# Moving the first burst of level products of the recurrence from index 52 to index 26 of its stage

## The chip, the cores and the metric

The kernel runs on one core of a Trainium2 chip. The metric is device time in microseconds (us) of one execution; several executions of the same program are timed and their median is compared. A profile of one execution shows when each instruction ran on each engine: PE (TensorE, the matrix engine; its weight loads are listed as PEld), DVE (VectorE), ACT (ScalarE), POOL (GpSimd) and SP (SyncE, which issues most transfers).

## The reference

The reference is one layer of a streaming encoder on a sequence of 256 positions and a model width of 1,024, in fp32. In order: a feed-forward block, a mixing block, a cross-attention to a memory of 256 positions, and a second feed-forward block, each with RMS norms and a residual. The change lies in the mixing block. One input projection makes the inputs of two branches. Branch A is a gated linear recurrence over 8 heads of 128 by 128 state:

```
def step(state, xs):
    qt, kt, it, bt = xs
    diff = bt[:, :, :, None, :] - bt[:, :, None, :, :]
    decay = jnp.exp(jnp.where(mask, diff, -jnp.inf))
    a = jnp.einsum('bhtd,bhsd,bhtsd->bhts', qt, kt, decay)
    o_intra = jnp.einsum('bhts,bhsv->bhtv', a, it)
...
o_a = rmsnorm(o_a.astype(x.dtype), hg_norm_g[l]) * jax.nn.silu(g_a)
```

Each score of query t and key s is weighted, channel by channel, by the product of the gates f between s and t. Branch B is an attention with a forget gate per head, whose logits f_b are eight columns of the same input projection. Both branches are projected, gated, added and projected out.

## The kernel before, in words

**Products in three parts.** An fp32 matrix product is made of three products of a reduced type: every operand is split into a high part and a low part. A weight tile (128 x 1024, or 128 x 688 for the columns spoken of here) is brought by SP into one of four buffers called raw; ACT rounds it into a tile called hi (line 145); DVE makes lo = raw - hi (line 147). SP can load the next tile into a raw buffer once DVE has made lo of the tile that was in it. hi and lo have eight buffers each.

**The stage of the change.** From about 252 us the kernel multiplies the normalized input by the columns of g_a and f_b (the loop at line 1023). They come in three groups of 344 columns, each of four weight tiles; a group is made for two halves of the positions, 24 products each, so the stage has 6 x 24 = 144 products of 128 x 344. They are indexed from 0 behind the mark r0. At the end of each half ACT makes a sigmoid (tile z, line 1030) and DVE multiplies it into G (line 1031). The two accumulators (tiles named mm) alternate, so a half can begin when DVE has made G of the half before the last one. Behind the stage come the products of k_b and q_b with 128 x 1024 weight tiles.

**Level products.** In the same time the recurrence is prepared. Its score matrix is built from levels: level 0 holds blocks of 1, and level m pairs blocks of m positions whose distance is covered by a product of gates. For two groups of four heads (class Rec, line 878) four methods act on a level: products (line 901) issues many small matrix products on PE, 32 x 32 or 32 x (2 x 16); grow (line 952) multiplies gates into the tiles k and qf on DVE (line 970) and combines gates (line 980), with copies on ACT of the early halves of k (gather, tile early, line 946) and of the later halves of qf (stash, into tile q, line 950); keep (line 990) copies the wanted part of the products into aux on DVE (lines 994 and 999) or on ACT. POOL clears parts of f after the first grow.

**Order.** Instructions of an engine run in the order in which they stand. The level work is taken out of the program order by hand: `after(i)` places all that it holds behind the matrix product with index i, with high priority, and a scheduler puts the ACT, DVE and POOL instructions into their queues accordingly. The levels come in six bursts, SETS = (0, 1), (2, 4), (8, 16), (32), (64), (128), and R_AT holds their six places:

```
for si, ms in enumerate(SETS):
    with after(r0 + R_AT[si]):
```

The first burst holds the products of levels 0 and 1 for both groups of heads (96 small products in the program; each is two matrix instructions, and each of these has a weight load), the grow of level 1 and the keep of both levels. The grow of level 2 stands behind the G of the second group's first half (R_GROW) whatever R_AT is.

Of the kernel before, what the change touches and what calls it, by code (L numbers as in the profile page):

```python
# [50 lines left out]
M_T = (106, 119)  # L51
M_O = (136, 140)

R_AT = (52, 126, 210, 252, 286, 318)

R_GROW = ((1, 0), (2, 1))

# [23 lines left out]
def block_kernel(ctx: ExitStack, tc: tile.TileContext, wts, head_in, gf_in, x_in, mem_in, memT_in, cols, rows, fbias, masks, out):  # L81
# [15 lines left out]
    @contextmanager  # L97
    def after(i):

        with tc.high_priority(), tc.issue_after(log[min(i, len(log) - 1)]):  # L100
            yield
# [13 lines left out]
    def acc():  # L115
        return pp.tile([P, 512], F32, tag="acc", name=nm("acc"), bufs=4)
# [968 lines left out]
    for si, ms in enumerate(SETS):  # L1085
        with after(r0 + R_AT[si]):
            banks = [acc()]
# [469 lines left out]
```

## Time and profile before

| what | us |
|---|---|
| median of 3 runs | 780.2 (780.06 to 780.88) |
| the profiled execution, its own time | 779.74 |
| its span, from first to last instruction | 777.5 |
| PE busy in the span | 766.7 |
| DVE, ACT, POOL busy in the span | 636.9, 490.4, 16.0 |

The profiled execution's own time is 2.24 us over its span, and 0.46 us under the median. In the profile's rows, a timeline row is start, length, engine, line, operation, output <- inputs, shape and count; a bracket holds the idle time before it and what ended it. A row of a table by stage is the stage, its length, then busy time and number of instructions of PE, PEld, DVE, ACT and POOL, the granted clock of PE, the share of the transfer engines and the rate. A row of a transfer queue is packets, megabytes and the share of sixteen transfer engines' time. "issue" is idle time of an engine for which the profile shows no releaser.

### The profile page before, as it was taken

To read this page: it belongs to the slowest core of one execution; us is meant where nothing else is said; L and a number is where in the kernel's file an instruction comes from. 1 tells how busy PE (TensorE), PEld (TensorE's weight loads), DVE (VectorE), ACT (ScalarE), POOL (GpSimd) and SP (SyncE) were. 2 spreads that over 40 slices of the span, in tenths; PEclk is the share of its full clock that TensorE was granted. 3 is DMA by queue.
4 is the path that set the end of the run, shared out by engine and by line. 5 is a ranking of instruction groups with operands and counts; after the bars stand their busy time and mean duration, and the time that the engine had idled before them with its cause. 6 is when DMAs were issued, how large, how long until landed. Compare 5 with 4: busy or idle time off the path is not lost.

```text
span 777.5 us, 11945 instructions
## 1 busy us (share of the span) xinstructions
PE 766.7 (99%) x4454; PEld 656.2 (84%) x4454; DVE 636.9 (82%) x989; ACT 490.4 (63%) x807; POOL 16.0 (2%) x39
## 2 busy tenths in 40 slices
PE   9999999999999899999999999999999999999996
PEld 8888888888888798898888888889888888888885
DVE  7798998988678799889776665885578688999993
ACT  7666565768675478557676444862768556565762
POOL 0000000000000101100000000000000000000000
PEclk9999999999999999999999999999999999999998
DMA  9739386365744534834666545456075536458241
GB/s 356 258 146 327 116 301 230 109 211 172 246 154 129 183 137 146 305 121 151 229 244 250 205 162 174 164 177 230 21 250 185 201 109 247 188 204 309 71 146 55
DMA packets 44506, 148.08 MB, mean 190 GB/s; under 512 B 5144, under 2 KB 8864, under 8 KB 44448
## 3 DMA queue, kind: packets, MB, share of 16 engines
q1 hardware_dynamic: 43168, 144.83, 52.5%
q0 software_dynamic: 848, 2.12, 1.1%
q8 instruction: 35, 0.57, 0.3%
q10 hardware_dynamic: 432, 0.37, 0.1%
q14 instruction: 23, 0.19, 0.1%
HBM read 146.24 MB, written 1.06 MB: 189 GB/s over the span
## 4 chain that ended last, share of the span: by engine, by line
PE 99%; issue 1%; DVE 0%; DVEq 0%; ACT 0%; ACTq 0%
PE mm L95 43%; PE acc L95 40%; PE tr L95 13%; PE tr L377 1%; PE tr L436 1%; PE tr L1194 0%; PE tr L1288 0%; PE acc L1407 0%; DVE xs L413 0%; DVE post L408 0%; DVEq L1552 0%; ACT junk L285 0%; DVE t L320 0%; PE tr L1045 0%; DVE y L322 0%
## 5 line engine op out<-in xcount | busy, mean ns | idle before, releaser
L147 DVE TENSOR_TENSOR lo<-raw,hi 128x1024 fp32r<-128x1024 f32 (+1 forms) x220 | 261.1, 1202 | 43.8 <-ACT hi L145 37.7
L145 ACT CAST hi<-raw 128x1024 fp32r<-128x1024 f32 (+1 forms) x220 | 223.7, 1035 | 76.2 <-PE mm L95 37.4
L95 PE MATMUL mm<-hi,hlT 128*128 128x512 f32 (+1 forms) x544 | 165.9, 382 | 3.4 <-issue 3.4
L95 PEld LDWEIGHTS mm<-hi,hlT 128*128 128x128 f32 x544 | 101.4, 190 | 20.3 <-issue 3.7
L95 PE MATMUL acc<-hi,act 128*128 128x512 f32 x352 | 113.2, 390 | 0.0
L95 PE MATMUL mm<-lo,hlT 128*128 128x512 f32 (+1 forms) x272 | 102.6, 382 | 0.0
L95 PEld LDWEIGHTS acc<-hi,act 128*128 128x128 f32 x352 | 66.1, 188 | 13.5
L95 PE MATMUL acc<-lo,act 128*128 128x512 f32 x176 | 69.2, 393 | 0.0
L95 PE MATMUL acc<-hlT,hi 128*128 128x512 f32 x272 | 68.7, 393 | 0.0
L95 PE MATMUL mm<-hlT,hi 128*128 128x512 f32 (+1 forms) x256 | 60.1, 365 | 0.0
L95 PEld LDWEIGHTS mm<-lo,hlT 128*128 128x128 f32 x272 | 51.6, 190 | 8.2 <-DVE lo L147 0.2
L95 PEld LDWEIGHTS acc<-hlT,hi 128*128 128x128 f32 x272 | 48.9, 189 | 8.7
L165 ACT CAST hi<-sraw 128x1024 fp32r<-128x1024 f32 x40 | 41.5, 1054 | 16.6 <-DVE sraw L573 10.7
L95 PEld LDWEIGHTS mm<-hlT,hi 128*128 128x128 f32 x256 | 44.9, 189 | 6.5
L166 DVE TENSOR_TENSOR lo<-sraw,hi 128x1024 fp32r<-128x1024 f32 x40 | 48.4, 1218 | 0.1
L95 PE MATMUL tr<-hlT,hi 128*128 128x512 f32 x176 | 44.6, 393 | 0.0
L95 PEld LDWEIGHTS acc<-hlT,lo 128*128 128x128 f32 x272 | 37.2, 190 | 2.7
L95 PEld LDWEIGHTS acc<-lo,act 128*128 128x128 f32 x176 | 33.1, 188 | 7.1 <-DVE lo L147 0.7
L95 PE MATMUL acc<-hlT,lo 128*128 128x256 f32 x272 | 38.4, 283 | 0.0
L95 PE MATMUL mm<-hlT,lo 128*128 128x256 f32 x224 | 36.6, 284 | 0.0
L95 PEld LDWEIGHTS tr<-hlT,hi 128*128 128x128 f32 x176 | 31.5, 189 | 5.6
L95 PEld LDWEIGHTS mm<-hlT,lo 128*128 128x128 f32 x224 | 32.5, 190 | 2.0
(294 smaller groups left out, 1270.7 us busy)
## 6 DMA issues: line engine op xcount, KB each, us to landing
raw<-in_wts_dram SPq DMA_DIRECT2D x231, 512.0 KB, 4.3
sraw<-in_wts_dram SPq DMA_DIRECT2D x16, 512.0 KB, 6.0
raw<-in_gf_dram SPq DMA_DIRECT2D x12, 344.0 KB, 3.8
head<-in_head_dram SPq DMA_DIRECT2D x7, 392.0 KB, 6.5
grow<-in_rows_dram SPq DMA_DIRECT2D x4, 512.0 KB, 5.3
xs<-in_x_dram SPq DMA_DIRECT2D x2, 512.0 KB, 7.8
cbm<-cd POOLq DMA_DIRECT2D x2, 512.0 KB, 8.0
brow<-in_rows_dram SPq DMA_DIRECT2D x4, 256.0 KB, 3.5
```

Source lines behind the costliest of these rows:

```text
L95: log.append(PE.matmul(*args, **kw).ins)
L145: S.copy(h, r)
L147: V.tensor_tensor(out=l, in0=r, in1=h.bitcast(F32), op=ALU.subtract)
L165: a = S.copy(hi, src)
L166: b = V.tensor_tensor(out=lo, in0=src, in1=hi.bitcast(F32), op=ALU.subtract)
L377: PE.transpose(blocks[-1][1], src(kb), ident)
L436: PE.transpose(trv[:, j, h * P : (h + 1) * P], ats[c, h][:, j * P : (j + 1) * P], ident)
```

## The change

One number is changed. The first burst stands behind index 26 of the stage instead of index 52; the five other bursts keep their places.

```
-R_AT = (52, 126, 210, 252, 286, 318)
+R_AT = (26, 126, 210, 252, 286, 318)
```

So the burst stands behind the third product of the first group's second half, where it stood behind the fifth product of the second group's first half. In the queues this moves the following, all of it by the scheduler:

- PE: the 96 small products stand 26 large products earlier. The program has the same products.
- DVE: the grow and keep of the burst (four multiplications, line 970, and four predicated copies, lines 994 and 999) stood behind the four lo tiles of the third weight group and the second G; now they stand ahead of these, and the first G stands between the first two multiplications.
- ACT: two early copies and two q copies stood behind the four hi tiles of the third group and the second z; now three of them stand ahead of the first of those hi tiles and one behind it.
- POOL and SP: the order of instructions is the same. The POOL clears wait for the early copies, and the next four SP loads (first weight tiles of k_b) wait for the four lo tiles that were moved.

## The prediction

> **What bounds the kernel now.** I read the page first, then the chain of waits near the burst, PE's timeline, stages, and the transfers. The page:
>
> ```profile
> span 777.5 us, 11945 instructions
> PE 766.7 (99%) x4454; PEld 656.2 (84%) x4454; DVE 636.9 (82%) x989; ACT 490.4 (63%) x807; POOL 16.0 (2%) x39
> ...
> q8 instruction: 35, 0.57, 0.3%
> ```
>
> PE sets the time: it is busy 99% of the span. The pieces of the chain around the burst:
>
> ```profile
> 252.34 8.36 PE mm L95 x53
> 260.70 1.81 PE acc L95 x129
> 262.51 1.78 PE mm L95 x10
> 264.29 3.38 issue
> 267.67 11.90 PE mm L95 x64
> ```
>
> Ten products after the burst PE stands idle for 3.38 us, with no releaser. PE's timeline, and stages beside it:
>
> ```profile
> 252.17 0.32 PE L95 MATMUL mm<-hi,hlT 128*128 128x344 f32 x1
> ...
> 260.38 0.32 PE L95 MATMUL mm<-lo,hlT 128*128 128x344 f32 x1
> 260.63 1.29 PE L95 MATMUL acc<-q,k 128*32 128x32 f32 x126
> ...
> 263.97 0.32 PE L95 MATMUL mm<-hi,hlT 128*128 128x344 f32 x1
> 267.67 0.42 PE L95 MATMUL mm<-hi,hlT 128*128 128x344 f32 x1 [3.38 <-issue]
> ```
>
> ```profile
> 0.00:260.60 260.60, 259.81 (x1297) 220.93 (x1297) 225.64 (x333) 173.88 (x272) 3.99 (x13) 1.00 0.60 212
> 0.00:261.26 261.26, 260.47 (x1369) 221.56 (x1373) 226.22 (x334) 174.50 (x272) 3.99 (x13) 1.00 0.61 212
> 0.00:264.20 264.20, 263.41 (x1499) 224.26 (x1499) 229.16 (x338) 175.93 (x275) 4.12 (x14) 1.00 0.61 213
> 267.60:271.50 3.90, 3.83 (x14) 3.84 (x15) 0.46 (x1) 0.55 (x1) 0.00 (x0) 0.56 0.02 6
> ```
>
> A product of the stage takes (260.38 - 252.17) / 52 = 0.158 us, start to start. Idle: 263.97 + 0.158 = 264.13 to 267.67, 3.54 us. Behind it the granted clock is 0.56 and 14 products take about 3.84 us where 14 x 0.158 = 2.21: 1.63 us more. The stall costs 3.54 + 1.63 = 5.17 us. What ends it is seen in the transfers, here in two windows, 250.3 to 265.2 and 265.2 to 266.3:
>
> ```profile
> q1 hardware_dynamic: 1571, 3.20, 61.5%
> ```
>
> ```profile
> q1 hardware_dynamic: 78, 0.26, 60.4%
> q8 instruction: 1, 0.02, 5.4%
> ```
>
> Queue q8 feeds PE with instructions: 0.57 MB for 4,454 + 4,454 instructions is 64 bytes each, and 35 refills make 8,908 / 35 = 255 instructions a refill. None came from 250.3 to 265.2. The one that then came lasted 5.4% x 16 x 1.1 = 0.95 us, to about 266.2, and PE went on 1.4 us later. PE had issued 1,499 + 1,499 = 2,998 instructions when it ran dry. One block earlier is 2,743, a count passed inside the burst, at 261.26 (1,369 + 1,373 = 2,742). So I read: there PE began its last block and asked for the next one; the burst eats nearly 400 instructions in 1.8 us, and the refill began 4.0 us after being asked for, behind weight transfers. PE ran dry first.
>
> **The change part by part.** PE's moved products: the same 192 small matrix instructions (1.81 us in the chain), 26 x 0.158 = 4.1 us earlier, from 260.63 to 256.52. Price 0. Three things must hold.
>
> First, their inputs. DVE's rows:
>
> ```profile
> 256.51 1.22 DVE L957 TENSOR_TENSOR qf<-q,f 128x1024 f32<-128x1024 f32 x1
> 257.66 0.57 DVE L1031 SCALAR_TENSOR_TENSOR G<-mm,facs,z 128x344 f32<-128x344 f32 x1
> 258.14 2.54 DVE L147 TENSOR_TENSOR lo<-raw,hi 128x688 fp32r<-128x688 f32 x3
> ...
> 261.25 0.88 DVE L147 TENSOR_TENSOR lo<-raw,hi 128x688 fp32r<-128x688 f32 x1
> 262.04 1.29 DVE L970 TENSOR_TENSOR k<-k,f 128x512 f32<-128x512 f32 x2
> 263.24 1.29 DVE L970 TENSOR_TENSOR qf<-qf,f 128x512 f32<-128x512 f32 x2
> 264.44 0.77 DVE L994 COPY_PREDICATED aux<-masks_s,acc 128x256 f32<-128x256 int32 x2
> 265.11 0.72 DVE L999 COPY_PREDICATED aux<-masks_s,acc 128x128 f32<-128x128 int32 x2
> 271.04 0.57 DVE L1031 SCALAR_TENSOR_TENSOR G<-mm,facs,z 128x344 f32<-128x344 f32 x1 [5.21 <-ACT z L1030]
> ```
>
> and ACT's moved copies, and the stage with the next weight transfers:
>
> ```profile
> 262.76 1.29 ACT L946 COPY early<-k 128x512 f32<-128x512 f32 x2 [1.55 <-DVE k L970]
> 263.96 1.25 ACT L950 COPY q<-qf 128x512 f32<-128x512 f32 x2
> ```
>
> ```profile
> 260.00:264.00 4.00, 4.00 (x207) 3.74 (x205) 3.92 (x7) 2.44 (x5) 0.00 (x0) 1.00 0.89 331
> ```
>
> The last input is the second qf: 256.51 + 1.22 = 257.73. Only the last sixth of the burst reads it, which PE reaches at 256.52 + 5/6 x 1.81 = 258.03. Margin 0.3 us; I take 0, and if it is gone PE waits for what is missing, some tenths.
>
> Second, the queues that it passes. DVE does 1.20 + 1.20 + 0.67 + 0.72 = 3.8 us of burst work (by starts, last copy whole) from 257.66 with the first G (0.48) between, until 261.9; then the four lo tiles. ACT's four copies (2.5 us) wait for those multiplications, three stand ahead of the first hi tile, which follows at about 260.6; the lo tiles end at about 265.6 instead of 262.13. Their first reader is product 96, which without a stall starts at 252.17 + 96 x 0.158 + 1.9 = 269.2: cover 3.6 us or more. The second G, now at 264.3 to 264.8, lets product 72 start, which comes at 265.5: cover 0.7 us. SP's next four loads start with the first lo, 3.7 us later (259.0 to 262.7). The four, of 0.52 MB each, take 2.1 MB / 331 GB/s = 6.3 us, until 270 with their start-up; product 144 needs them at 252.17 + 144 x 0.158 + 1.9 = 276.8 or later, with hi and lo made in between: cover some us. POOL's clears come earlier and nobody waits for them soon.
>
> Third, the refill. Instruction 2,743 stands 2,743 - 2,594 = 149 behind the count at 260.60 and 52 deeper in the moved burst, 201 of about 384: 256.5 + 0.9 = 257.4. From there to the start of the refill the nearest rows bound it: 1.1 us (the refill after the stall, when nothing else is moving: PE enters a block at 267.67, and the refill fills 5.4% of 268.7 to 269.8) and 4.0 us (the one above, behind transfers). Two windows show the traffic: the first is 268.7 to 269.8, the second 259 to 260.
>
> ```profile
> q8 instruction: 1, 0.02, 5.4%
> ```
>
> ```profile
> q1 hardware_dynamic: 16, 0.02, 5.0%
> ```
>
> The third group's transfers die out at 259 (5.0% in that microsecond), and the next train, which held the refill back, now starts after 262.7. I take 259.0, between 258.5 and 261.4. With 0.95 and 1.4 us the block can be used from 261.4 (260.9 to 263.8). PE has done the same work at the same time as before, so it would run dry at 264.1. Even the slow end is in time. The stall goes: -5.17 us. The half clock goes with it, as it followed the idle time.
>
> [...]
>
> What is late next: DVE. It idled 5.21 us behind the stall, and it was at full speed while PE was at half clock. When the G of product 71 is made, PE has gained only the idle time and about two thirds of the slow stretch; DVE, contiguous from there, stays some 0.5 us later against PE. The place with least cover, where PE's seventh low-part product ends the row and the lo tile must be there:
>
> ```profile
> 311.07 1.22 DVE L147 TENSOR_TENSOR lo<-raw,hi 128x1024 fp32r<-128x1024 f32 x1
> ```
>
> ```profile
> 311.92 1.00 PE L95 MATMUL mm<-hlT,lo 128*128 128x256 f32 x7
> ```
>
> The tile is ready at 312.29, read at 311.92 + 1.00 - 0.28 = 312.64. Cover 0.35 - 0.5 leaves PE about 0.2 us of wait (0 to 0.5). Sum: -5.17 + 0.2 = -5.0. Against the profiled execution 779.74 - 5.0 = 774.7; its median is 0.46 higher, so 780.2 - 5.0 = 775.2.
>
> **The rivals.**
>
> The refill comes too late again in part. For it: transfers of the third group still run when it is asked for, and its delay is known from two cases only. Against it: they stop at 259. It decides from a delay of 264.1 - 2.35 - 257.4 = 4.35 us on. A delay of 6.5 us leaves 2.2 us of idle time and perhaps half of the 1.63: -5.0 + 3.0, 778.2.
>
> [...]
>
> Slower, by a later refill. The k_b loads start 3.7 us later, so their 6 us train lies on 263.8 to 270, where the refill after the next is asked for (about 261.4 to 264). It has to start by 272 to be usable at 274.6, where the second burst (267.67 + 11.90 = 279.57 before, less 5.2, plus some tenths) empties that block. Behind a train it starts at about 270, 2 us in time. Only from about 276 on, if a second train were joined to the first, would idle time (3.5 us) and half clock (1.6) eat the gain; started at 279 it leaves 6.8 us idle and 1.6 at half clock: 775.2 + 8.4 = 783.6.
>
> **How the numbers follow.** Forecast 0.75 (774.6 to 775.9: the wait of 0 to 0.5, the qf margin, and the runs' own spread); late in part 0.12 (776 to 779.5); no change 0.08; slower 0.05. A difference within 0.2% (1.6 us) can't be told from none. Faster by more, under 778.6: 0.75 and most of the second, 0.86. Same 0.09, slower 0.05. The time is 775.2. The range leaves out no change, slower and the worse half of the second case, under 0.2: 774.5 to 777.6.
>
> **What would show it.** Right: no issue idle behind the first burst, a granted clock of 1.0 from 252 to 284, a q8 refill at 258.5 to 261.5, DVE without the 5.21 us, the product behind the burst 5 us earlier from 272 on, some tenths of wait near 307. Wrong: idle time of PE inside the burst (its inputs), ten or so products behind it (no refill question at all), or after the second burst.

## The result, and the profile after

The changed kernel took 777.22 us in the median of 5 runs (776.83 to 778.32), beside 780.56 us (780.06 to 781.53) for the kernel before in the same runs: a ratio of 0.9959, 95% interval 0.9944 to 0.9974. It is faster, by 3.3 us where the sum gave 5.0. The profiled execution took 776.83 us.

The page of the changed kernel:

```profile
span 774.6 us, 11943 instructions
PE 766.7 (99%) x4454; PEld 654.9 (85%) x4454; DVE 636.3 (82%) x989; ACT 489.5 (63%) x807; POOL 15.8 (2%) x39
```

PE is busy for the same 766.7 us; what has gone is idle time. The chain of waits around the burst (start, length, what), and four stages:

```profile
253.49 4.26 PE mm L95 x27
257.75 1.81 PE acc L95 x133
259.57 7.31 PE mm L95 x45
```

```profile
252.00:260.20 8.20, 8.20 (x234) 7.87 (x233) 7.30 (x11) 4.08 (x7) 0.00 (x0) 1.00 0.56 172
260.20:261.30 1.10, 1.10 (x9) 1.10 (x8) 1.10 (x3) 0.69 (x3) 0.00 (x0) 1.00 0.08 25
260.60:264.20 3.60, 3.60 (x25) 3.60 (x24) 3.56 (x8) 3.58 (x6) 2.46 (x12) 1.00 0.02 5
264.20:268.00 3.80, 3.80 (x26) 3.80 (x26) 3.03 (x5) 2.08 (x5) 0.19 (x1) 1.00 0.78 259
```

PE is busy for the whole of every stage, at a granted clock of 1.00. Behind the burst stand 7.31 us of products without a break, where there were 1.78 us, the 3.38 us of "issue" and a spell at 0.56. The transfer queue between 260.2 and 261.3 us shows the refill that was late before:

```profile
q8 instruction: 1, 0.02, 5.0%
q1 hardware_dynamic: 14, 0.01, 3.0%
```

It comes as the third group's transfers have died out. The next loads are issued later than before: SP's row of the kernel before and then of the changed one.

```profile
259.04 3.44 SPq L143 DMA_DIRECT2D raw<-in_wts_dram  x4
```

```profile
263.84 3.29 SPq L143 DMA_DIRECT2D raw<-in_wts_dram  x4
```

DVE has lost its 5.21 us of idle time; 0.77 us are left:

```profile
262.90 2.61 DVE L147 TENSOR_TENSOR lo<-raw,hi 128x688 fp32r<-128x688 f32 x3
265.42 0.57 DVE L1031 SCALAR_TENSOR_TENSOR G<-mm,facs,z 128x344 f32<-128x344 f32 x1
265.91 0.87 DVE L147 TENSOR_TENSOR lo<-raw,hi 128x688 fp32r<-128x688 f32 x1
267.55 0.58 DVE L1031 SCALAR_TENSOR_TENSOR G<-mm,facs,z 128x344 f32<-128x344 f32 x1 [0.77 <-ACT z L1030]
```

Three pieces take back part of the 5.17 us. The stage itself begins later in this execution, at 253.33 instead of 252.17, and that lies ahead of the change; PE has a new wait for a lo tile at 309 us; and it waits for 0.18 us near the end.

```profile
253.33 0.32 PE L95 MATMUL mm<-hi,hlT 128*128 128x344 f32 x1
...
309.11 0.39 PE L95 MATMUL mm<-hlT,lo 128*128 128x256 f32 x1 [0.33 <-DVE lo L147]
...
752.71 0.50 PE L95 MATMUL acc<-hi,act 128*128 128x512 f32 x1 [0.18 <-ACT act L165]
```

### The profile page after: what moved, and what is told of

Its sections match the earlier page's. It is cut to its first block, busy times and chain, and to the rows that moved or that the text cites. A ratio compares the mean times of both kernels' runs of the same rounds, so it can differ in the third digit from the quotient of the medians.

```text
span 774.6 us, 11943 instructions
## 1 busy us (share of the span) xinstructions
PE 766.7 (99%) x4454; PEld 654.9 (85%) x4454; DVE 636.3 (82%) x989; ACT 489.5 (63%) x807; POOL 15.8 (2%) x39
## 4 chain that ended last, share of the span: by engine, by line
PE 89%; DVE 6%; ACT 2%; DMA 1%; issue 1%; DVEq 0%; ACTq 0%; SPq 0%
PE acc L95 38%; PE mm L95 38%; PE tr L95 11%; DVE lo L147 1%; DVE lo L166 1%; DMA raw<-in_wts_dram 1%; PE tr L377 1%; DVE k L970 1%; DVE qf L970 1%; PE tr L436 1%; ACT hi L165 1%; ACT f L1008 0%; PE tr L1194 0%; DVE sraw L573 0%; ACT hi L145 0%
```

## The experiments

Theory A is that of the prediction: PE runs dry a block of instructions (255, from 8,908 instructions in 35 refills) after a boundary, and an early request for the refill is enough. Rival B says that the gain comes from the train of k_b weights, which was held back, and rival C that the idle time belongs to the burst and its place. Two more questions came with the result: why the gain is 3.3 us and not 5, and what makes the new wait. Where a run has one time and no number of runs beside it, that is one execution.

### Is it the count of instructions?

Three kernels shift the block boundaries by small products in the warm-up, where PE waits for its first inputs, and one moves the burst to a third place.

**204 instructions more, burst at 52.**

```
-WARM = 8
+WARM = 3
...
         MM(wps[:, :P], one, one, start=True, stop=True)
+    for _ in range(56):
+        MM(wps[:32, :32], one[:32, :32], one[:32, :32], start=True, stop=True)
```

> The burst stays behind index 52; in the warm-up five of the eight large products are left out and 56 small ones added, 204 PE instructions more in all. The block boundary that lay 147 instructions into the burst then lies 57 ahead of it, the next 199 into it, as it does with index 26. Theory A (PE runs dry by the count of instructions between two refills): nothing stands ten products behind the burst any more; asked for at about 256 and 261.6, the refills are used from 261.4 to 262.5 and from about 267.6, where PE would run dry at 261.6 and 268.1, so 0 to 0.9 us of idle time in all, and about 775.5 to 777.5 us. Rival C (the idle time is tied to the burst and its place, not to a count): 3.5 us ten products behind the burst as before, about 780.

Measured: 781.72 us. The warm-up was dearer than thought: it takes 7.73 us where it took 3.76, and the burst starts at 266.34 instead of 260.63, 5.71 us late before anything is tested. The stages around the burst, and the first row of the count:

```profile
0.00:258.98 258.98, 258.03 (x1353) 218.32 (x1354) 218.30 (x322) 169.76 (x265) 3.99 (x13) 1.00 0.61 207
...
264.00:268.00 4.00, 4.00 (x206) 3.78 (x205) 3.21 (x5) 2.42 (x4) 0.00 (x0) 1.00 0.86 279
268.00:272.00 4.00, 4.00 (x50) 3.96 (x37) 4.00 (x9) 2.92 (x5) 1.40 (x7) 1.00 0.93 336
```

The idle time and the half clock are gone, with the burst at index 52 and the weight transfers at a share of 0.86 and 0.93 around it. So the idle time is not tied to the burst or its place: rival C falls. The total hides that, because 5.71 us were lost in the warm-up and 1.14 us more in a wait for a lo tile at 314 us: 779.74 + 5.71 - 5.17 + 1.14 = 781.4.

The count gives something new. In the transfer queue between 258.9 and 260.5 us the refill for the boundary at count 2,743 is already there:

```profile
q8 instruction: 1, 0.02, 5.5%
```

It begins at 258.98 us, when PE had executed 1,353 + 1,354 = 2,707 instructions, 36 short of the boundary. The prediction had put the request at the moment at which PE executes the boundary. It is made at least 36 instructions earlier.

**204 instructions more, burst at 26.** The same edit on the changed kernel.

> The burst stands behind index 26 as in the changed kernel; the same 204 PE instructions more in the warm-up put a block boundary 5 instructions ahead of the burst and the next one 251 into it. Theory A: the refill is asked for as the burst begins, and PE runs dry 1.2 us later, inside the burst; the refill can be used 3.45 us (1.1 + 0.95 + 1.4) or more after it was asked for, so 2.3 to 3.7 us of idle time inside the burst, behind some 125 of its 192 small matrix instructions, with a spell of lower clock behind it: 779.5 to 782.5 us. Rival C (the place of the burst decides): no idle time there, about 777 us.

Measured: 782.49 us, and no idle time in the burst. Theory A as it was worked out missed, and rival C had named this. But C has fallen with the run before, and the count tells what was wrong with A: the refill starts at 259.25, again at a count of 2,707, while the burst begins at 262.51. The 36 instructions ahead of this boundary are 18 stage products, 2.8 us, and that is enough. The 5.7 us over the changed kernel's profiled execution are the warm-up (the burst starts 262.51 - 257.68 = 4.8 us later) and a lo wait of 1.15 us at 314.75, 0.8 us longer. For PE to run dry the boundary has to lie deeper in the burst, so that the request falls into it too; the next run puts it there.

**104 instructions more, burst at 26.** As above with `WARM = 0` and 34 small products.

> As the run with 204 more instructions at index 26, but 104 more: 34 small products in the warm-up in place of its eight large ones, which should cost about the same time. The block boundary then lies about 95 instructions into the burst, the one before it 161 ahead of the burst. Theory A, with what the runs so far add (a refill starts before its boundary is executed, so it is asked for some 50 instructions ahead of execution): from the request, some 45 instructions into the burst, to running dry, 351 instructions into it, PE needs only (351 - 45) x 1.81 / 384 = 1.4 us, and the refill needs 0.8 us or more to start, 0.95 us to land, 1.4 us to be used: PE stands idle inside the burst, near its end, for at least 1.7 us, and for up to 3.3 us if the refill starts only when the third group's transfers have ended; with the lower clock behind it 779.5 to 782.5 us. If the count does not matter: no idle time, 777 us.

Measured: 779.89 us. PE's timeline of this run:

```profile
258.53 1.29 PE L95 MATMUL acc<-q,k 128*32 128x32 f32 x126
...
259.67 0.61 PE L95 MATMUL acc<-qf,early 128*32 128x32 f32 x46
263.15 0.34 PE L95 MATMUL acc<-qf,early 128*32 128x32 f32 x16 [2.87 <-issue]
```

PE stops for 2.87 us inside the burst with 16 of its 192 small matrix instructions left, that is behind the 176th; 351 instructions, half of them weight loads, had been named. No tile and no engine is waited for. The count from the start to 262.5 us, in the middle of this idle time:

```profile
0.00:262.50 262.50, 259.48 (x1499) 219.85 (x1499) 225.30 (x332) 172.55 (x270) 4.30 (x14) 1.00 0.61 210
```

PE stops after 1,499 + 1,499 = 2,998 instructions, the same count as in the kernel before, though that is another place of the program now. Instructions added 250 us earlier bring the stall back at index 26, at the place that the count gives. The spell of lower clock that was expected behind it did not come.

**The burst at 40.**

```
-R_AT = (26, 126, 210, 252, 286, 318)
+R_AT = (40, 126, 210, 252, 286, 318)
```

> The first burst behind index 40. The block boundary then lies 147 + 2 x 12 = 171 instructions into the burst and the next one 427 behind its start, 43 behind its end: the place where PE can run dry moves from ten products behind the burst to 21 or 22. Of the lo tiles of the third weight group two stand ahead of the burst's DVE work and two behind it, so two of the k_b loads start early and are on their way when the refill is asked for. From the request (some 50 instructions ahead of the boundary) to running dry PE has 263 x 1.81 / 384 + 21 x 0.158 = 4.6 us; the refill needs 0.95 us to land and 1.4 us to be used, so it is late if it starts more than 2.2 us after the request. Delays seen under transfers are 1.8 to 5.2 us. Theory A: idle time, if there is any, stands 21 or 22 products behind the burst and lasts 0 to 3 us, less than with 52; the median lies between the two kernels, 777 to 779.5 us. Rival C (idle time belongs to the burst's place): ten products behind it, or nothing.

Measured: 777.71 us (7 runs, 776.62 to 777.87), 0.9958 of the kernel before (0.9942 to 0.9974). PE's timeline behind the burst:

```profile
261.31 0.58 PE L95 MATMUL mm<-hi,hlT 128*128 128x344 f32 x2
261.73 0.32 PE L95 MATMUL mm<-lo,hlT 128*128 128x344 f32 x1
...
264.57 0.32 PE L95 MATMUL mm<-lo,hlT 128*128 128x344 f32 x1
264.73 0.65 PE L95 MATMUL mm<-hi,hlT 128*128 128x344 f32 x2
265.22 0.31 PE L95 MATMUL mm<-lo,hlT 128*128 128x344 f32 x1
```

The third product behind the burst starts at 261.73, so the one at 264.73 is number 3 + (264.73 - 261.73) / 0.158 = 22. A pair like this takes 0.48 us elsewhere (first and second 0.158 us apart); here it takes 0.65, so the second came 0.17 us late. PE ran dry behind 22 products, where the count put it; at 264.85 us the count is again 1,499 + 1,499. Index 40 is just about far enough in this execution.

### Does the transfer train delay the refill?

**The train held back, burst at 52.** Four raw buffers are taken by a one-column memset that stands behind the burst's DVE work.

```
+    held = [wp.tile([P, D], F32, tag="raw", name=nm("held"), bufs=4) for _ in range(4)]
+    with tc.high_priority(), tc.issue_after(gf_last[1, 0]):
+        for t in held:
+            V.memset(t[:, 0:1], 0.0)
```

> The burst stays behind index 52; the loads of the first four k_b tiles wait in addition for a one-column memset behind the burst's DVE work, so their train starts at about 266 instead of 260. The block boundary stays 147 instructions into the burst. Theory A with B (the refill is late because the train is in its way): asked for at 261.3, it starts 1.1 to 1.9 us later, at 262.4 to 263.2, can be used from 264.8 to 265.6, and the idle time ten products behind the burst falls from 3.5 us to 0.6 to 1.5 us. If the train is not what delays it: 3.5 us as before. Not read from this run is the total: the k_b tiles come 6 us late and PE may wait for them at about 272 to 277.

Measured: 779.04 us. The loads are issued at 268.58 instead of 259.04. The count at the boundary, PE's row behind the burst, and the transfers in 261.8 to 263.1 and in 263.1 to 264.2 us:

```profile
0.00:262.31 262.31, 260.64 (x1369) 221.04 (x1373) 226.30 (x334) 174.82 (x272) 3.98 (x13) 1.00 0.61 210
```

```profile
265.55 0.42 PE L95 MATMUL mm<-hi,hlT 128*128 128x344 f32 x1 [0.21 <-issue]
```

```profile
DMA packets 0, 0.00 MB, mean 0 GB/s; under 512 B 0, under 2 KB 0, under 8 KB 0
```

```profile
q8 instruction: 1, 0.02, 5.5%
```

The refill starts at 263.1, 0.8 us after PE has executed count 2,742 at 262.31, instead of 4.0, and the idle time falls from 3.38 to 0.21 us. A rest is still there, at the same ten products: at this place even a refill with the queue to itself is a little late. The train made the other 3.2 us, measured against the profile that the prediction used; against the three further profiles of the kernel before, which stand below, it is 1.1 to 4.1 us. That it is 0.21 and not 0.6 to 1.5 us agrees with the earlier request.

**Products alone moved.** The products stand behind 26; grow and keep are put behind the last hi and lo of the third weight group.

```
+            with tc.issue_after(behind[0]) if si == 0 else nullcontext():
+              with tc.issue_after(behind[1]) if si == 0 else nullcontext():
...
                         r.grow(ms[-1])
...
                     r.keep(m, LEVELS.index(m) if m < 64 else None)
```

> Only the small products of the first burst stand behind index 26; its grow and keep on DVE and its copies on ACT stay behind the lo and hi tiles of the third weight group, as with 52. So the train of k_b weights starts at about 260 us, as before, and not 3.7 us later. Theory A (it is enough that the refill is asked for early): asked for at about 257.5, it starts by about 259.5, in the gap between the two trains; no issue idle behind the burst, PE's clock stays at 1.00. Rival B (the gain comes from holding back the train): the refill starts only behind the train, at about 265, and PE stands idle for about 3.5 us before 267.7 as before.

Measured: 783.77 us. There is no issue idle behind the burst, but the run does not tell A from B as it was meant to: behind the moved products the hi tiles of the third group come later (DVE waits 1.64 us for the first), the lo tiles with them, and the train was issued at 261.66, not at 259.04. In 260.3 to 261.4 us the refill has the queue nearly to itself, as in the changed kernel:

```profile
q8 instruction: 1, 0.02, 5.0%
q1 hardware_dynamic: 9, 0.01, 2.5%
```

The run with 204 instructions more at 52 answers the question instead: an early request is enough. The total of this run is bad for another reason: with grow late, DVE makes the lo tiles of k_b late, and PE waits for one for 3.18 us at 286.36.

### What does the stall cost?

**The kernel before, three more times.**

> The kernel before once more, for a second profile of it. Of 22 further runs of it, 7 have a mean clock of 0.998 or more and took 779.1 us in the mean, 15 have 0.997 or less (0.995 in the profile of before) and took 780.7. Theory G (the price of the stall changes from execution to execution: the clock drops in some of them only): the idle time ten products behind the burst is there every time, but between 1.5 and 3.6 us long with the refill starting 4.3 to 2.4 us after the request; where it is under 3 us (2.9 us in the run with 104 instructions more left the clock at 1.00), no half clock follows. Theory H (the stall is 5.17 us each time, and the change loses 1.5 to 2 us elsewhere in the median): 3.5 us and the half clock each time.

> The same again, for a third profile. Theory G: idle time and spell of half clock differ between these profiles. Theory H: they are the same in each.

> The same again, for a fourth profile. Theory G: at least one of the four profiles of this kernel has a shorter stall or no spell of half clock. Theory H: all four have 5.2 us.

Measured: 780.31, 782.94 and 779.18 us. For the first, the second and the third of them, each time PE's timeline at the product ten behind the burst, and then the stage of 3.9 us from there:

```profile
267.37 0.42 PE L95 MATMUL mm<-hi,hlT 128*128 128x344 f32 x1 [1.29 <-issue]
```

```profile
267.30:271.20 3.90, 3.83 (x24) 3.83 (x25) 1.78 (x5) 1.71 (x3) 1.41 (x7) 1.00 0.16 61
```

```profile
269.41 0.50 PE L95 MATMUL mm<-hi,hlT 128*128 128x344 f32 x1 [4.35 <-issue]
```

```profile
269.30:273.20 3.90, 3.79 (x14) 3.79 (x15) 0.32 (x1) 0.55 (x1) 0.00 (x0) 0.56 0.02 6
```

```profile
267.05 0.53 PE L95 MATMUL mm<-hi,hlT 128*128 128x344 f32 x1 [1.86 <-issue]
```

```profile
267.00:270.90 3.90, 3.85 (x15) 3.85 (x16) 0.36 (x1) 0.55 (x1) 0.86 (x5) 0.56 0.07 24
```

The stall is there every time, at the same product, but its length is 1.29, 4.35 and 1.86 us beside 3.38 in the profile that the prediction used. In the first one no spell of lower clock follows: 24 products in 3.83 us. By the working of the prediction (0.16 us more of idle time, and what the products take over 0.158 us each) the four cost 1.29 + 0.16 = 1.45, 4.35 + 0.16 + 1.58 = 6.09, 1.86 + 0.16 + 1.48 = 3.50, and 5.17: 4.05 us in the mean. Theory G holds in that the price changes from execution to execution, and theory H falls. G's details missed: 1.29 and 4.35 us lie outside its 1.5 to 3.6, and 1.86 us, under its 3, did bring the lower clock.

### The new wait

**The changed kernel again.**

> The changed kernel once more, beside the next ones on the same chip. Same median as before within 0.1%, 776.8 to 778. If the first products start by scatter, the 0.9 us that its first profile lost against that of the kernel before in the first 9 us come out differently here; if the place of the burst had a part in it, they are the same.

Measured: 777.02 us (11 runs, 775.79 to 778.63) beside 779.79 us (22 runs, 778.16 to 782.83), a ratio of 0.9957 (0.9943 to 0.9971). Its stage begins at 252.65; in the three further profiles of the kernel before it begins at 253.96, 252.94 and 253.07. So the 1.16 us by which the stage began later in the first profile of the changed kernel are not of the change: the kernel before alone spreads over 1.8 us there (252.17 to 253.96). The wait for the lo tile is there again:

```profile
308.61 0.39 PE L95 MATMUL mm<-hlT,lo 128*128 128x256 f32 x1 [0.52 <-DVE lo L147]
```

**The last burst at 317.**

```
-R_AT = (26, 126, 210, 252, 286, 318)
+R_AT = (26, 126, 210, 252, 286, 317)
```

> The changed kernel with the last burst behind index 317 instead of 318, that is ahead of the second half's last but one low-part product. Theory D (the new wait of 0.3 to 0.55 us near 309 us is for one lo tile only): the 1.95 us of the burst cover it, no wait for a lo tile there, 0.3 to 0.6 us less than the changed kernel, about 776.8. Rival: the wait moves to the next low-part product or to the burst's own inputs, and the time stays.

Measured: 775.65 us (6 runs, 774.34 to 777.19), 0.9949 of the kernel before (0.9932 to 0.9966). PE's timeline there has no wait:

```profile
307.38 0.88 PE L95 MATMUL mm<-hlT,lo 128*128 128x256 f32 x6
308.09 1.95 PE L95 MATMUL acc<-qf,k 128*128 128x128 f32 x16
309.80 0.48 PE L95 MATMUL mm<-hlT,lo 128*128 128x256 f32 x2
```

The burst runs while the lo tile is made: theory D. The median is the lowest of all the kernels, 1.4 us under the changed kernel in the same runs, more than the 0.5 us of the wait; the two intervals overlap, so what the profile shows is shown, and the rest is not.

**Keep late.** The four predicated copies of the first burst go behind the third group's lo tiles.

```
+            with tc.issue_after(behind) if si == 0 else nullcontext():
...
                     r.keep(m, LEVELS.index(m) if m < 64 else None)
```

> The changed kernel, but the keep of the first burst (four predicated copies, 1.4 us of DVE) stands behind the four lo tiles of the third weight group again; its grow stays ahead of them. The lo tiles and with them the loads of k_b come 1.4 us earlier; DVE's work in all is the same. Theory E (the tile at 309 us is late because its weights come late, since raw buffers came free late): the wait there shrinks by some tenths or goes, 776.7 to 777.0. Theory F (DVE's queue itself is late): the wait stays at 0.3 to 0.6 us and the time at 777.2. The first burst's refill is asked for at the same time and starts before the train: no idle time behind it in either case.

Measured: 777.58 us (12 runs, 775.94 to 778.68), 0.9968 of the kernel before (0.9957 to 0.9979). The wait stays, 0.39 us; on DVE the lo tile begins at 308.34, as the work ahead of it ends, while its hi was ready at 306.99 + 1.05 = 308.04. The run by itself is a weak test of E, because the edit moved the loads less than was meant: they are issued 263.93 - 253.77 = 10.16 us behind the start of the stage, and 10.51 in the changed kernel, 0.35 us earlier and not 1.4, since DVE waited 0.80 us for a hi tile there. What decides is the two rows at the tile itself: earlier weights would not have let DVE begin before 308.34. So it is DVE's queue that is late (theory F), and not the weights (E). The kernel before shows the same wait, 0.86 us, in the profile in which its stall was short and its clock full, and in none of its three others. It is a wait that the stall had covered.

## Why the prediction was right, and where it was wrong

Times of the changed kernel's first profile are given here less the 1.16 us by which its stage begins later.

- **What bounds the kernel: right.** The idle time comes from the refill. It followed the count into the burst, to 22 products behind it and away altogether. The change does two things to it, an earlier request and a later train; the run with 204 instructions more at 52 shows that the first alone removes the stall, and the run with the train held back that the second alone leaves 0.21 us of it.
- **The burst's inputs: right.** Neither the burst nor the products behind it wait. A margin of 0.3 us held.
- **The queues that it passes: right.** DVE began the lo tiles at 261.7 (261.9 was given) and ended them at 265.6 (265.6); the next loads were issued at 262.7 (262.7); no reader of these tiles waited before 309 us.
- **The refill: the time right, the request wrong.** It starts at about 259.1 (259.0). But it is not asked for where PE executes the boundary, at a count of 2,743: in the two runs with 204 instructions more it starts at 2,707, 36 instructions earlier, so it is asked for there or before. At index 26 this changes nothing. In the run with 204 instructions more at 26 it turned an expected stall into none. What sets the 36 no run here shows.
- **What the stall costs: the step that failed.** "The stall costs 3.54 + 1.63 = 5.17 us" was read from one execution and set against a median. Four profiles give 1.45 to 6.09 and 4.05 in the mean. The mechanism was right, and the term 1.1 us too large by that mean; four values that lie so far apart fix it to about 1 us only (an estimate from their spread, 2.0 us over the root of 4).
- **What is late next: right in place and cause, too small.** 0.2 us was taken (0 to 0.5); it was 0.33 and 0.52 in the two profiles of the changed kernel, and up to 1.15 in other kernels without the stall. One step on the way was wrong: DVE is not contiguous from the G of product 71 on. In the changed kernel it waits for ACT's kp at 297.55 (0.58 us) and for ACT's plo at 301.49 (0.45 us), in the kernel before for 0.67 and 0.46 us, and in both the lo tile begins 6.35 us behind the second of these waits. So ACT has a part in the new wait; how large a part was not tried.
- **The sum.** 4.05 - 0.4 = 3.6 us, where 5.0 was forecast and the medians differ by 3.3 and, in the second series, by 2.8. The few tenths that are left are within the scatter of the runs, 1.5 us and more for each kernel. 777.2 us lies in the range given, at its upper end, and outside the likeliest case's own range (774.6 to 775.9). The range reached so far because it had room for a refill late in part, which did not happen; that the time fell inside it is to that extent luck.
- **The rivals.** The refill was not late again; the refill after it, which would have made the change slower, begins at 263.71 us in the changed kernel, just ahead of the loads issued at 263.84, and PE did not wait for it. No change, given 0.08, is refuted by the ratio of 0.9959 (0.9944 to 0.9974); the idle time is tied to the count of instructions and not to the burst, since 204 more of them took it away with the burst at 52.

## What to carry to other kernels

Idle time of PE with no releaser, inside a dense burst or a few products behind it, is worth holding against the instruction queue's refills: count the instructions, find the block boundary that lies in the burst (here PE stood still 2,998 - 2,743 = 255 instructions behind it), and move the burst, or the count, or the transfers that stand in the refill's way. Instructions added 250 us ahead made such a stall here (104 of them, 2.87 us at index 26) and unmade it (204, at index 52), so a kernel with dense bursts is to be looked at again after every edit. And a term that depends on a race between transfers (1.29 to 4.35 us of idle time here) is to be read from several executions before it is set against a median.

## What the runs showed of the hardware that was not expected

- **The lower clock does not follow the length of the idle time alone.** After 1.86, 3.38 and 4.35 us of idle time PE ran at a granted 0.56 over the next 3.9 us; after 1.29 us, and after 2.87 us in the run with 104 instructions more, at 1.00 throughout. By the working above, the products behind 1.86 us of idle time took 1.48 us more than at 0.158 us each, and those behind 2.87 us ran at full clock. So 1.86 us of idle time cost more behind them than 2.87 us did. What decides whether the clock falls was not tried.

- **The stall's length varies threefold between executions of one program**, 1.29 to 4.35 us at the same product. Transfers were under way in the two stalls in which their share was read: 0.56 over 264.00 to 267.60 us in the profile that the prediction used, 0.96 over 266.00 to 267.37 us in the first further one. What spreads the refill's delay was not tried.
